# Output projection of a hybrid decoder layer: w_out held in SBUF, x of two quarters kept for the norm, additions on GpSimd, transposes laid between the products

## The chip, the cores and the metric

One core of a Trainium2 chip runs the whole layer. The metric is the device time of one execution in microseconds; the median over the runs of a kernel is given, with the lowest and the highest. A profile is one further execution that the hardware profiler took; its span and its own time stand beside the median below.

## The reference

One decoder layer on x of 2048 rows (tokens) by 1024 columns, all in float32. What matters here are its last steps:

```python
mixed = jnp.concatenate([attn, conv], axis=-1)
x = x + g1 * (mixed @ w_out)

h2 = rmsnorm(x, norm2_g) * (1 + sc2) + sh2
u = causal_dwconv(h2 @ w_up, ffn_conv_w)
u_gate, u_val = jnp.split(u, 2, axis=-1)
y = (jax.nn.silu(u_gate) * u_val) @ w_down
return x + g2 * y
```

`mixed` is 2048 x 1024 (512 columns of attention, 512 of a short convolution), `w_out` 1024 x 1024, `w_up` 1024 x 5632, `w_down` 2816 x 1024. The vectors g1, sc2, sh2, g2 come from the conditioning input and are the same for all rows.

## The kernel before, in words

**Products.** Every float32 product is made of three TensorE matmuls: an operand is split into a high part `hi` (ScalarE, "ACT", L845) and the rest `lo = raw - hi` (VectorE, "DVE", L846), and `mm3` (L139) adds hi·hi, lo·hi and hi·lo into one PSUM accumulator. A matmul here is 128 x 128 by 128 x 512.

**Stages.** The profiled execution runs the projections and the convolution first, then attention (until about 979 us), then the stage of this change, the output projection, until 1208 us, and then the feed-forward part: `up(0)` (1208 to 1634 us), `down` for two quarters, `up(1)`, `down` for the other two.

**The output projection** is `mixed(Q)`, L858, called for four quarters Q of 512 rows. Each has two halves `hf` of 512 output columns. A half goes through eight slices k of 128 rows of w_out, in the order 4, 5, 6, 7, 0, 1, 2, 3; for each k it loads a slice of w_out (L868, 256 KB) into a raw tile (4 buffers), and the matching piece of `mixed`: for k of 4 and over, high and low parts that an earlier stage wrote to DRAM (`m_hi`, `m_lo`, L873 and L874), straight into a pair tile (4 buffers of hi, 4 of lo, taken in turn, so a load waits until TensorE has used the k four places earlier); for k under 4 the attention's output (`m_at`, L870), unsplit. Then come twelve products, three for each of four row tiles t. k = 2 and k = 3 are taken together, t by t. So a half is 96 products in four accumulators, which have four buffers: the next half's accumulator t is the same bank as this one's.

**What follows a half** is `add_gated` (L849) for each t: a load of x (L852), accumulator times gate on DVE (L854), the addition on DVE (L855), the store of the result to x1 in DRAM (L856). Its tiles x and g come from `temp()`, six buffers of 128 x 512 in turn, which all the small steps of this part of the kernel share.

**The norm** `norm2(Q)` (L893) reads x1 of a quarter back (L899), squares it on ACT (L901), scales it on DVE (L906), and for each of eight column blocks makes four transposes on TensorE (L911) and one ACT operation (`columns`, L913). From these come the operands of the up projection: for an even quarter b11 and b21, for an odd one, joined with the even one's by sums and differences on DVE, b22, t1, t2, t3 and t4 (seven products instead of eight). The order is mixed(0), mixed(1), norm2(0), mixed(2), norm2(1), mixed(3), up(0); norm2(2) and norm2(3) lie in `down`.

**The up projection** `up(hv)` (L977) has 22 pairs of column blocks; each pair is seven calls of `product` (L988), twelve matmuls each, in the order b11, t2, b21, t1, t3, b22, t4, into three accumulators X, Y, Z. Between them an accumulator is copied out before the next product is added to it.

**What orders the work.** The program is written in one order, and a scheduler lays the instructions out on each engine by their priority and by when it expects them to be ready; what is wrapped in `K(...)`, like the products of up, keeps its place in the program. In `mixed` the last argument of `mm3`, False, leaves the products free. All loads and stores are issued by SP, one queue.

## Time and profile before

| | |
|---|---|
| median of 3 runs (lowest to highest) | 2562.1 us (2558.01 to 2565.7) |
| profiled execution: its own time, its span | 2563.71 us, 2562.0 us |
| mean granted TensorE clock | 0.988 |
| TensorE busy (matmuls) | 2461.8 us, 96% of the span |
| DVE, ACT, GpSimd busy | 71%, 45%, 12% |
| output projection, 979.65 to 1208.2 us | 228.55 us, TensorE busy 197.21 of it, granted clock 0.93, DMA engines busy 0.83 |
| up(0), 1208.2 to 1634.5 us | 426.3 us, TensorE busy 421.88 of it |

A window's row gives its length, then for each engine the busy time and the number of instructions, then the granted clock as a share of full speed (PEclk), the mean busy share of the sixteen DMA engines, and GB/s. A busy time counts matmuls at whatever clock was granted, so a slow clock does not show as idle time. A row of the waits says which engine and line waited, for which engine (or DMA) and line, how long in total, how often, and the longest. In a timeline a row is a start, a duration, the engine, the line, the instruction and, in brackets, the idle time before it with what ended it; "SPq" rows are issues of DMAs. PE is TensorE, POOL is GpSimd.

### The profile page before, as it was taken

Reading aid. Unit: us, or ns where it says so; the run is one execution under the profiler, and the core shown is the slowest. Engines: PE = TensorE matmul, PEld = TensorE weight load, DVE = VectorE, ACT = ScalarE, POOL = GpSimd, SP = SyncE. Lnnn points to the kernel's source line nnn. Section 1 sums busy time; section 2 is a strip of 40 time slices with the busy share of each in tenths; the row PEclk is TensorE's granted clock in tenths of the full one; section 3 lists DMA queues with packets and bytes.
Section 4 is the critical chain, followed back from the end, with each engine's and each line's share of the span. In section 5 each row is a group of like instructions: output and inputs, shape, how many; then the busy total and the mean of one; then the engine's idle time right before and its main releaser. Section 6 shows DMA issues by size and latency. Waiting matters only on the chain.

```text
span 2562.0 us, 38669 instructions
## 1 busy us (share of the span) xinstructions
PE 2461.8 (96%) x14474; PEld 2030.1 (79%) x14474; DVE 1819.8 (71%) x3266; ACT 1154.9 (45%) x1880; POOL 309.6 (12%) x266
## 2 busy tenths in 40 slices
PE   4999999999999998897999999999999999999999
PEld 4988888887888887675888888877778888888887
DVE  7567874443888884568788888766758888885554
ACT  3532231112888883244444444455434444444333
POOL 4211010112656650000000000000000000000000
PEclk9999999999999999998999999999999999999999
DMA  8433674316799958886222222676642222226776
GB/s 233 144 116 101 194 217 119 118 64 172 141 207 183 178 116 262 298 297 193 83 83 83 83 82 83 201 221 213 215 144 83 83 87 86 75 90 193 224 235 186
DMA packets 423203, 395.97 MB, mean 155 GB/s; under 512 B 136208, under 2 KB 312680, under 8 KB 419944
## 3 DMA queue, kind: packets, MB, share of 16 engines
q1 hardware_dynamic: 415960, 380.86, 51.8%
q10 hardware_dynamic: 7056, 12.65, 1.4%
q8 instruction: 113, 1.85, 0.3%
q14 instruction: 74, 0.61, 0.1%
HBM read 286.41 MB, written 77.66 MB: 142 GB/s over the span
## 4 chain that ended last, share of the span: by engine, by line
PE 51%; DVE 3%; DMA 1%; ACT 1%; issue 1%; SPq 0%; ACTq 0%; DVEq 0%
PE acc L988 33%; PE acc L139 17%; DVE lo L846 1%; DMA raw<-m_at 0%; PE pt L911 0%; DMA t<-x_sc 0%; DVE t L854 0%; DVE t L855 0%; ACT hi L845 0%; DMA t<-in_x_dram 0%; DMA hi<-m_hi 0%; ACT junk L901 0%; ACT t L913 0%; DVE t4l L846 0%; DVE b22l L846 0%
## 5 line engine op out<-in xcount | busy, mean ns | idle before, releaser
L846 DVE TENSOR_TENSOR lo<-raw,hi 128x1024 fp32r<-128x1024 f32 (+1 forms) x240 | 275.4, 1153 | 252.5 <-ACT hi L845 250.3
L845 ACT ACTIVATE hi<-raw 128x1024 fp32r<-128x1024 f32 (+1 forms) x240 | 239.4, 1002 | 375.7 <-PE acc L139 240.6
L139 PE MATMUL acc<-hi 128*128 128x512 f32 x960 | 377.6, 397 | 27.0 <-DVE t L854 11.6
L139 PE MATMUL acc<-lo,hi 128*128 128x512 f32 x960 | 381.0, 397 | 7.6 <-DVE lo L846 7.4
L139 PE MATMUL acc<-hi,lo 128*128 128x512 f32 x960 | 379.7, 396 | 1.5 <-DMA lo<-m_lo 1.5
L1001 DVE SCALAR_TENSOR_TENSOR w<-w,fcw,w 128x1024 f32<-128x1024 f32 x176 | 225.9, 1283 | 35.4 <-ACT w L996 32.1
L139 PEld LDWEIGHTS acc<-hi 128*128 128x128 f32 x960 | 182.3, 190 | 70.5 <-DVE t L854 14.9
L940 ACT ACTIVATE hi<-raw 128x1024 fp32r<-128x1024 f32 x132 | 139.7, 1060 | 211.2 <-PE acc L988 203.0
L139 PEld LDWEIGHTS acc<-lo,hi 128*128 128x128 f32 x960 | 182.6, 190 | 48.1 <-DVE lo L846 11.2
L139 PEld LDWEIGHTS acc<-hi,lo 128*128 128x128 f32 x960 | 183.0, 191 | 40.8 <-DMA lo<-m_lo 3.5
L943 DVE TENSOR_TENSOR lo<-raw,hi 128x1024 fp32r<-128x1024 f32 x132 | 161.0, 1221 | 13.2 <-ACT hi L940 13.2
L704 ACT ACTIVATE s_t<-s_t,nb 128x2048 f32<-128x2048 f32 (+15 forms) x128 | 152.9, 1196 | 5.7
L139 PE MATMUL pr<-hh,wh 128*128 128x512 f32 x384 | 153.3, 399 | 0.0
L139 PE MATMUL pr<-hl,wh 128*128 128x512 f32 x384 | 151.0, 393 | 0.0
L139 PE MATMUL pr<-hh,wl 128*128 128x512 f32 x384 | 150.7, 392 | 0.0
L731 DVE TENSOR_TENSOR near<-pt,near 128x512 f16<-128x512 f32 (+1 forms) x192 | 115.0, 600 | 43.7 <-ACT near L726 42.8
L663 PE MATMUL ps<-kh,qs 128*128 128x512 f32 (+1 forms) x320 | 133.8, 419 | 1.9 <-DVE mx L687 1.1
L687 DVE CUSTOM_DVE_ANT_0 s_t<-ps,nf,mx 128x512 f32<-128x512 f32 (+1 forms) x192 | 123.2, 642 | 2.6
L716 POOL TENSOR_TENSOR wide<-s_t,wide 128x896 f16<-128x896 f32 x64 | 121.5, 1899 | 5.4
L664 PE MATMUL ps<-kl,qs 128*128 128x512 f32 (+1 forms) x320 | 115.5, 365 | 0.0
L724 PE MATMUL pt<-ident,s_t 128*128 128x128 f32 x640 | 101.2, 283 | 6.8 <-DVE near L731 4.4
L139 PE MATMUL acc<-wh,hh 128*128 128x512 f32 x256 | 103.3, 404 | 0.0
(272 smaller groups left out, 6109.0 us busy)
## 6 DMA issues: line engine op xcount, KB each, us to landing
raw<-in_w_up_dram SPq DMA_DIRECT2D x88, 512.0 KB, 3.6
raw<-y_sc SPq DMA_DIRECT2D x176, 256.0 KB, 3.9
raw<-in_w_down_dram SPq DMA_DIRECT2D x176, 256.0 KB, 4.3
y_sc<-w SPq DMA_DIRECT2D x44, 512.0 KB, 2.6
wm<-in_w_ada_dram SPq DMA_DIRECT2D x128, 128.0 KB, 2.7
raw<-in_w_out_dram SPq DMA_DIRECT2D x64, 256.0 KB, 5.7
wr<-in_w_in_dram SPq DMA_DIRECT2D x40, 256.0 KB, 4.2
x_t<-in_x_dram SPq DMA_DIRECT2D x16, 512.0 KB, 5.2
```

What stands on the lines that cost most here:

```text
L139: ins = T.matmul(acc, lhsT=a, rhs=b, start=st, stop=sp)
L663: K(T.matmul(ps[:, 0:cw], lhsT=qt, rhs=kh[:, c0 : c0 + cw], start=True, stop=False))
L664: K(T.matmul(ps[:, 0:cw], lhsT=qt, rhs=kl[:, c0 : c0 + cw], start=False, stop=not last))
L687: K(V.tensor_tensor_reduce(out=s_t[:, o0 + c0 : o0 + c0 + cw], in0=ps[:, 0:cw], in1=nf[:, c0 : c0 + cw], scale=1.0, scalar=-3.0e38 if g == ...
L704: K(A.activation(cols, cols, AF.Exp, bias=nb[:, p : p + 1], accum_out=un["l"][:, p : p + 1]))
L716: K(G.tensor_tensor(wide[:, 1, :], s_t[:, WB * P : WU], wide[:, 0, :], op=ALU.subtract))
L845: A.activation(hi, raw, AF.Copy, scale=HS)
L846: V.tensor_tensor(lo, raw, hi.bitcast(F32), op=ALU.subtract)
L940: K(A.activation(hi, raw, AF.Copy, scale=HS))
L943: K(V.tensor_tensor(lo, raw, hi.bitcast(F32), op=ALU.subtract))
L988: K(T.matmul(acc, lhsT=a, rhs=b, start=st, stop=sp, skip_group_check=True))
L1001: K(V.scalar_tensor_tensor(y, u[:, m : m + 1024], fcw[:, m * 44 + ct : m * 44 + ct + 1], y, op0=ALU.mult, op1=ALU.add))
```

## The change

- **w_out is loaded once.** In mixed(0) the sixteen slices of 128 x 512 (4 MB) go into tiles of a new pool `fb`, which have the names and the buffers that the operands b22 and t4 take later; the other quarters split from there (L847, L848). k under 4 now has two splits of 512 columns, one for w_out and one for m_at, instead of one of 1024, and m_at (L882) is loaded into a tile of `temp()`.
- **x is kept.** The x of quarters 0 and 1 is loaded into four raw tiles and four wide tiles, and the addition is made there in place, so that norm2(0) and norm2(1) read no x1 back. The store to x1 stays.
- **GpSimd** makes the additions of mixed (L858) and the scaling of the norms of quarters 0 and 1 (L943). `temp()` has seven buffers.
- **The products of mixed and the transposes keep their place in the program.** norm2 is a generator now; mixed(1) takes a step of norm2(0) after its first k and then after each k from the sixth on, counted over both halves, and mixed(2) does so with norm2(1).
- **b22 and t4 of quarter 1** need the buffers that hold w_out, so they come after mixed(3): `norm2_rest(1)` makes four steps in the first pair of up(0), after the products b11, t2, b21 and t1, each with four transposes (of columns that mixed(2) has already used for t2 and t3, made a second time), one column on ACT, a split, three operations on DVE for t4 (two before), and a split. norm2(3) makes t4 with the same three operations.

The scheduler then lays out the queues anew from the start of mixed on; before it they are the same. On SP, in the first half of Q1, there stood before (m_at_73 and m_at_74 are k = 2 and 3 of this half, m_hi_75 is the first k of the next; in brackets stands whom an entry waits for, DMAHW being the queues' own counters):

```order
L870 DMA raw<-m_at_73 128x512 [waits DMAHW4_49]
L868 DMA raw<-in_w_out_dram 128x512 [waits DMAHW5_49,Activation_49]
L870 DMA raw<-m_at_74 128x512 [waits DMAHW6_49]
L852 DMA t_13892<-in_x_dram 128x512 [waits DMAHW7_49]
L868 DMA raw<-in_w_out_dram 128x512 [waits DMAHW0_49,DVE_49]
L868 DMA raw<-in_w_out_dram 128x512 [waits DMAHW2_49,DMAHW1_49,DVE_49]
L873 DMA hi<-m_hi_75 128x512 [waits PE_49]
```

All m_at of the half stand ahead of the next half's m_hi. In the same half of the change, on SP (m_hi_76 is the second k of the next half):

```order
L885 DMA hi<-m_hi_75 128x512 [waits DMAHW5_49,DVE_49,PE_49]
L886 DMA lo<-m_lo_79 128x512 [waits DMAHW6_49]
L885 DMA hi<-m_hi_76 128x512 [waits DMAHW7_49,DVE_49,PE_49]
L882 DMA t_13919<-m_at_73 128x512 [waits DMAHW0_49]
L886 DMA lo<-m_lo_80 128x512 [waits DMAHW1_49]
L882 DMA t_13938<-m_at_74 128x512 [waits DMAHW2_49]
```

The m_at of k = 2 and k = 3 have moved behind two m_hi that wait for TensorE. At the end of the first half of Q2 there stands now on SP (m_hi_78 is the fourth k of the next half; the t tiles take x):

```order
L885 DMA hi<-m_hi_78 128x512 [waits DMAHW1_49,DVE_49,PE_49]
L855 DMA t_14462<-in_x_dram 128x512 [waits DMAHW2_49]
L855 DMA t_14468<-in_x_dram 128x512 [waits DMAHW3_49]
L855 DMA t_14474<-in_x_dram 128x512 [waits DMAHW6_49,DMAHW4_49]
L886 DMA lo<-m_lo_82 128x512 [waits DMAHW5_49]
L859 DMA x_sc_91<-t_14462 128x512 [waits Pool_49]
L859 DMA x_sc_92<-t_14468 128x512 [waits DMAHW7_49,Pool_49]
L859 DMA x_sc_93<-t_14474 128x512 [waits DMAHW0_49,Pool_49]
L855 DMA t_14480<-in_x_dram 128x512 [waits DMAHW1_49,DVE_49]
```

The x of the half that ends have moved behind the last m_hi of the next one, where before the first of them stood ahead of the next half's first m_hi. And on ACT, in the first pair of up(0) (t_15154 is the first deferred column, L1073 the copy of the accumulator X):

```order
L918 ACTIVATE t_15154<-pt,sh_141,a_140 128x512 [waits DMAHW1_49,PE_49,Pool_49]
L847 ACTIVATE b22h<-t_15154 128x512 [waits Activation_49]
L847 ACTIVATE t4h<-t_15160 128x512 [waits DVE_49]
L1073 ACTIVATE t_15169<-acc 128x512 [waits DMAHW7_49,DMAHW4_49,Pool_49]
L1078 ACTIVATE w_15171<-halo 128x2
L918 ACTIVATE t_15192<-pt,sh_141,a_140 128x512 [waits DMAHW5_49,PE_49,Pool_49]
```

The copy of X, which before had none of these in front of it, now stands behind the column and two splits.

The diff, cut to its core:

```diff
+NTEMP = 7
...
+        fb = ph.enter_context(tc.tile_pool(name="fb", bufs=1))
...
-        def add_gated(acc, gate, src, dst):
-
-            xp = temp()
+        def add_gated(acc, gate, src, dst, xp=None, eng=V):
+
+            if xp is None:
+                xp = temp()
             nc.sync.dma_start(xp, src)
             g = temp()
             V.tensor_tensor(g, acc, gate, op=ALU.mult)
-            V.tensor_tensor(xp, xp, g, op=ALU.add)
+            eng.tensor_tensor(xp, xp, g, op=ALU.add)
             nc.sync.dma_start(dst, xp)
 
-        def mixed(Q):
+        wo, kept = {}, {}
+
+        def mixed(Q, side=iter(()), wait=0):
 
             cols = slice(Q * 512, (Q + 1) * 512)
+            n = 0
+            if Q == 0:
+                kept[0] = [raw_tile() for _ in range(4)]
+                kept[1] = [wide_temp()[:, 0:D] for _ in range(4)]
             for hf in range(2):
                 n0 = hf * 512
                 acc = [ps_d.tile([P, 512], F32, tag="d", name="acc") for _ in range(4)]
                 ops = []
                 for k in (4, 5, 6, 7, 0, 1, 2, 3):
-                    raw, tiles = raw_tile(), pair_tiles()
-                    (mh, ml), (wh, wl) = halves(tiles)
-                    nc.sync.dma_start(raw[:, 512:1024], w_out[k * P : (k + 1) * P, n0 : n0 + 512])
+                    if Q == 0:
+                        wo[k, hf] = fb.tile([P, 512], F32, tag=f"{('b22', 't4')[k // 4]}{k % 4}{'hl'[hf]}", name="wo")
+                        nc.sync.dma_start(wo[k, hf], w_out[k * P : (k + 1) * P, n0 : n0 + 512])
+                    (mh, ml), (wh, wl) = halves(pair_tiles())
+                    split(wo[k, hf], wh, wl)
                     if k < 4:
-                        nc.sync.dma_start(raw[:, 0:512], m_at[k][:, cols])
-                        split(raw, *tiles)
+                        raw = temp()
+                        nc.sync.dma_start(raw, m_at[k][:, cols])
+                        split(raw, mh, ml)
                     else:
                         nc.sync.dma_start(mh.bitcast(F32), m_hi[k - 4][:, cols])
                         nc.sync.dma_start(ml.bitcast(F32), m_lo[k - 4][:, cols])
-                        split(raw[:, 512:1024], wh, wl)
                     ops.append((mh, ml, wh, wl))
                     for t in () if k == 2 else range(4):
                         for o in ops:
                             a, b = [m[:, t * P : (t + 1) * P] for m in o[:2]]
-                            mm3(acc[t], a, b, *o[2:], k == 4, o is ops[-1] and k == 3, False)
+                            mm3(acc[t], a, b, *o[2:], k == 4, o is ops[-1] and k == 3)
                     if k != 2:
                         ops = []
+                    n += 1
+                    if n == 1 or n > wait:
+                        next(side, None)
                 for t in range(4):
                     r = Q * 4 + t
-                    add_gated(acc[t], gates[:, n0 : n0 + 512], x[r * P : (r + 1) * P, n0 : n0 + 512], x1_sc[r][:, n0 : n0 + 512])
+                    xp = kept[Q][t][:, n0 : n0 + 512] if Q < 2 else None
+                    add_gated(
+                        acc[t], gates[:, n0 : n0 + 512], x[r * P : (r + 1) * P, n0 : n0 + 512], x1_sc[r][:, n0 : n0 + 512], xp, G
+                    )
 
         bt = {}
 
         def operand(name, k, raw):
-            bt[name, k] = [fp.tile([P, 512], F32R, tag=f"{name}{k}{e}", name=f"{name}{e}") for e in "hl"]
+            pool = fb if name in ("b22", "t4", "t3") else fp
+            bt[name, k] = [pool.tile([P, 512], F32R, tag=f"{name}{k}{e}", name=f"{name}{e}") for e in "hl"]
             split(raw, *bt[name, k])
...
+        xn = {}
+
+        def columns(Q, k):
+            pt = ps_n.tile([P, 512], F32, tag="n", name="pt")
+            for t in range(4):
+                K(T.transpose(pt[:, t * P : (t + 1) * P], xn[Q][t][:, k * P : (k + 1) * P], ident))
+            h = temp()
+            A.activation(h, pt, AF.Identity, bias=sh2[:, k : k + 1], scale=a2[:, k : k + 1])
+            return h
+
+        def last_operands(Q, k, b2):
+            b21, t2 = bt["b21", k], bt["t2", k]
+            operand("b22", k, b2)
+            t4, t5 = temp(), temp()
+            V.tensor_tensor(t4, b21[0].bitcast(F32), t2[0].bitcast(F32), op=ALU.subtract)
+            V.tensor_tensor(t5, b21[1].bitcast(F32), t2[1].bitcast(F32), op=ALU.subtract)
+            V.tensor_tensor(t4, t4, t5, op=ALU.add)
+            operand("t4", k, t4)
+
         def norm2(Q):
 
             ss = fp.tile([P, 16], F32, tag="ss", name="ss", bufs=2)[:, 0:4]
-            xn = []
+            xn[Q] = kept.get(Q) or [wide_temp()[:, 0:D] for _ in range(4)]
             for t in range(4):
-                xt = wide_temp()[:, 0:D]
-                nc.sync.dma_start(xt, x1_sc[Q * 4 + t])
-                junk = fp.tile([P, D], BF16, tag="t2", name="junk", bufs=6)
-                A.activation(junk, xt, AF.Square, accum_out=ss[:, t : t + 1])
-                xn.append(xt)
+                if Q >= 2:
+                    nc.sync.dma_start(xn[Q][t], x1_sc[Q * 4 + t])
+                junk = fp.tile([P, D], BF16, tag="t2", name="junk", bufs=NTEMP)
+                A.activation(junk, xn[Q][t], AF.Square, accum_out=ss[:, t : t + 1])
             V.tensor_scalar(ss, ss, 1.0 / D, EPS, op0=ALU.mult, op1=ALU.add)
             rsqrt(fp, ss, 4, "r")
             for t in range(4):
-                V.tensor_scalar(xn[t], xn[t], ss[:, t : t + 1], None, op0=ALU.mult)
-
-            def columns(k):
-                pt = ps_n.tile([P, 512], F32, tag="n", name="pt")
-                for t in range(4):
-                    T.transpose(pt[:, t * P : (t + 1) * P], xn[t][:, k * P : (k + 1) * P], ident)
-                h = temp()
-                A.activation(h, pt, AF.Identity, bias=sh2[:, k : k + 1], scale=a2[:, k : k + 1])
-                return h
-
+                if Q < 2:
+                    G.tensor_scalar(xn[Q][t], xn[Q][t], ss[:, t : t + 1], 0.0, op0=ALU.mult, op1=ALU.add)
+                else:
+                    V.tensor_scalar(xn[Q][t], xn[Q][t], ss[:, t : t + 1], None, op0=ALU.mult)
+            yield
             for k in range(4):
-                b1, b2 = columns(k), columns(4 + k)
                 if Q % 2 == 0:
-                    operand("b11", k, b1)
-                    operand("b21", k, b2)
+                    for n, name in enumerate(("b11", "b21")):
+                        operand(name, k, columns(Q, 4 * n + k))
+                        yield
                     continue
-                operand("b22", k, b2)
-                b11, b21 = [[e.bitcast(F32) for e in bt[n, k]] for n in ("b11", "b21")]
-                t1, t2, t3, t4 = [temp() for _ in range(4)]
+                b1 = columns(Q, k)
+                b11 = [e.bitcast(F32) for e in bt["b11", k]]
+                t1, t2, t3 = [temp() for _ in range(3)]
                 V.tensor_tensor(t1, b1, b11[0], op=ALU.subtract)
                 V.tensor_tensor(t1, t1, b11[1], op=ALU.subtract)
                 operand("t1", k, t1)
+                yield
+                b2 = columns(Q, 4 + k)
                 V.tensor_tensor(t2, b2, t1, op=ALU.subtract)
                 operand("t2", k, t2)
                 V.tensor_tensor(t3, b2, b1, op=ALU.subtract)
                 operand("t3", k, t3)
-                V.tensor_tensor(t4, b21[0], t2, op=ALU.subtract)
-                V.tensor_tensor(t4, t4, b21[1], op=ALU.add)
-                operand("t4", k, t4)
+                if Q == 3:
+                    last_operands(Q, k, b2)
+                yield
+
+        def norm2_rest(Q):
+            for k in range(4):
+                last_operands(Q, k, columns(Q, 4 + k))
+                yield
...
-        def up(hv):
+        def up(hv, side):
...
                 product(X, o11, "b11", True)
+                next(side, None)
...
                 product(Y, os2, "t2", True)
+                next(side, None)
...
                 product(X, o12, "b21", False)
+                next(side, None)
...
                 product(Z, os1, "t1", True)
+                next(side, None)
...
         mixed(0)
-        mixed(1)
-        norm2(0)
-        mixed(2)
-        norm2(1)
+        mixed(1, norm2(0), 5)
+        mixed(2, norm2(1), 5)
         mixed(3)
         for hv in range(2):
-            up(hv)
+            up(hv, iter(()) if hv else norm2_rest(1))
             for n in range(4):
                 down(2 * hv + n // 2, n % 2)
                 if hv == 0 and n < 2:
-                    norm2(2 + n)
+                    for _ in norm2(2 + n):
+                        pass
```

More of the change, by code (lines that the diff above doesn't have):

```diff
@@ L838, in temp @@
         def temp():
-            return fp.tile([P, 512], F32, tag="t2", name="t2", bufs=6)
+            return fp.tile([P, 512], F32, tag="t2", name="t2", bufs=NTEMP)
         def wide_temp():
```

## The prediction

> **What bounds the kernel now.** I read the page first, then windows cut at the ends of the halves of the output projection, then the waits of TensorE in that stage, then single timelines. The windows are the eight halves (Q0 first half, Q0 second half, and so on), and the whole stage last.
>
> ```profile
> core 0: us, PE busy (x) PEld busy (x) DVE busy (x) ACT busy (x) POOL busy (x), PEclk, DMA share, GB/s
> 979.65:1001.40 21.75, 21.75 (x92) 17.84 (x91) 9.51 (x11) 7.27 (x9) 0.00 (x0) 0.92 0.86 288
> 1001.40:1025.90 24.50, 22.66 (x97) 17.63 (x96) 12.64 (x17) 6.78 (x8) 0.00 (x0) 1.00 0.86 278
> 1025.90:1051.40 25.50, 22.94 (x97) 17.59 (x96) 12.24 (x16) 6.77 (x8) 0.00 (x0) 1.00 0.90 296
> 1051.40:1075.30 23.90, 22.68 (x97) 17.62 (x97) 11.55 (x15) 5.40 (x6) 0.00 (x0) 1.00 0.88 307
> 1075.30:1112.20 36.90, 28.88 (x129) 21.91 (x129) 23.97 (x44) 21.60 (x34) 0.00 (x0) 0.86 0.86 280
> 1112.20:1138.20 26.00, 23.27 (x98) 17.59 (x97) 12.03 (x17) 6.78 (x8) 0.00 (x0) 1.00 0.89 300
> 1138.20:1186.40 48.20, 33.23 (x138) 25.30 (x137) 43.88 (x79) 28.80 (x46) 0.00 (x0) 0.84 0.64 207
> 1186.40:1208.20 21.80, 21.80 (x94) 17.89 (x92) 12.22 (x16) 5.31 (x5) 0.00 (x0) 0.96 0.92 289
> ...
> 979.65:1208.20 228.55, 197.21 (x832) 153.37 (x830) 138.04 (x208) 88.70 (x124) 0.00 (x0) 0.93 0.83 273
> ```
>
> A half without gaps takes 21.8 us. Two halves, those with the norm between them, take 36.9 and 48.2. In 228.55 us TensorE is busy 197.2 and idle 31.3; the granted clock of 0.93 costs another 228.55 × 0.07 = 16. So 181 us is work at full clock, and 47 us could be won at most. Who makes TensorE wait (total, times, longest):
>
> ```profile
> PE acc L139 <- DVE t L854: 11.0, 3, 8.7
> PE acc L139 <- ACT hi L845: 7.9, 1, 7.9
> PE acc L139 <- DMA hi<-m_hi: 5.1, 5, 1.9
> PE acc L139 <- DVE lo L846: 4.4, 5, 2.9
> PE acc L988 <- DVE lo L943: 4.4, 1, 4.4
> ```
>
> The 8.7 and the 7.9 belong to the norms (DVE's chain, and Squares that wait for the reloaded x1). The last row is the first pair of the up projection. What a wait costs beside itself shows behind that one. The first two rows below are TensorE's timeline, the others windows of 3.4 us from there:
>
> ```profile
> 1208.10 0.39 PE L988 MATMUL acc<-b11l,hi 128*128 128x512 f32 x1
> 1212.91 0.79 PE L988 MATMUL acc<-b11h,lo 128*128 128x512 f32 x1 [4.42 <-DVE lo L943]
> ```
> ```profile
> 1211.60:1215.00 3.40, 2.09 (x5) 1.71 (x6) 3.24 (x5) 0.72 (x2) 0.00 (x0) 0.58 0.10 36
> 1215.00:1218.40 3.40, 3.40 (x9) 2.63 (x9) 2.36 (x2) 2.20 (x5) 0.00 (x0) 0.50 0.09 25
> 1218.40:1221.80 3.40, 3.40 (x15) 2.75 (x15) 0.68 (x2) 0.00 (x0) 0.00 (x0) 0.92 0.92 271
> ```
>
> After 4.42 us idle the clock is 0.58, 0.50 and 0.92 in three windows: (0.42 + 0.50 + 0.08) × 3.4 = 3.4 us lost again. I take 3.4 for waits of 4 to 6 us, and half, 1.7, for waits of 2 to 3 (an estimate).
>
> One more view decides the forecast: the timeline of SP, which issues all the loads, around 1138.2, where a half ends.
>
> ```profile
> 1130.88 0.32 SPq L873 DMA_DIRECT2D hi<-m_hi  x1
> 1131.25 0.42 SPq L874 DMA_DIRECT2D lo<-m_lo  x1
> 1131.73 1.25 SPq L852 DMA_DIRECT2D t<-in_x_dram  x1
> ...
> 1138.25 0.33 SPq L856 DMA_DIRECT2D x_sc<-t  x1
> 1138.67 0.38 SPq L873 DMA_DIRECT2D hi<-m_hi  x1
> ...
> 1140.84 1.03 SPq L856 DMA_DIRECT2D x_sc<-t  x2
> ...
> 1142.48 0.43 SPq L873 DMA_DIRECT2D hi<-m_hi  x1
> ```
>
> The m_hi load at 1130.88 goes into a pair tile (4 buffers, 8 k per half) and so waits until TensorE is through with the k four places earlier, 7.3 us before the half's end; the x load behind it goes out right after, never before. The m_hi of 1142.48 stands behind the stores of 1140.84. SP's queue is taken in order, and a load waits for the entries ahead of it.
>
> **The change part by part.** Prices:
>
> ```profile
> raw<-m_at SPq DMA_DIRECT2D x32, 256.0 KB, 5.0
> t<-in_x_dram SPq DMA_DIRECT2D x32, 256.0 KB, 3.7
> ...
> hi<-m_hi SPq DMA_DIRECT2D x28, 256.0 KB, 4.5
> ```
> ```profile
> L846 DVE TENSOR_TENSOR lo<-raw,hi 128x1024 fp32r<-128x1024 f32 x32 | 39.0, 1224 | 48.3 <-ACT hi L845 46.2 <-DMA raw<-in_w_out_dram 1.6
> ...
> L854 DVE TENSOR_TENSOR t<-acc,gates 128x512 f32<-128x512 f32 x32 | 21.9, 688 | 11.6 <-PE acc L139 11.5
> ...
> L845 ACT ACTIVATE hi<-raw 128x512 fp32r<-128x512 f32 x29 | 18.3, 630 | 44.3 <-PE acc L139 25.0 <-DMA raw<-in_w_out_dram 15.0 <-DMA t<-in_x_dram 4.1
> L913 ACT ACTIVATE t<-pt,sh,a 128x512 f32<-128x512 f32 x16 | 12.3, 768 | 3.3 <-PE pt L911 3.0 <-DMA raw<-m_at 0.3
> ```
> ```profile
> L274 POOL TENSOR_TENSOR hl<-hf,hh 128x512 fp32r<-128x512 f32 x8 | 10.4, 1297 | 0.7
> ...
> L263 POOL TENSOR_SCALAR x_t<-x_t,ss 128x1024 f32<-128x1024 f32 x2 | 3.2, 1604 | 2.6 <-DVE ss L126 2.6
> ```
>
> *What goes.* The w_out loads of Q1 to Q3 and the x1 reloads of two norms; the bulk of the norms' work is laid between products. The 7.9 and the 8.7, and the clock behind them, end. Work stays 181; the first half's clock (0.92 of 21.75 = 1.7) stays, and I leave 3 us for small waits at the ends of halves. Stage without new waits: 186. Splitting k < 4 in two pieces adds instructions on DVE and ACT, which are busy half of a half; the scalings (4 × 1.6 us, twice) lie on GpSimd, beside products. Both I cost at nothing; were the scalings late, transposes would wait about 1 us, in places where TensorE waits anyway.
>
> *What comes: m_at behind m_hi.* The first two groups of rows of SP's queue that stand with the change show Q1's first half. Before, all m_at of the half stood ahead of the next half's m_hi. Now m_hi_76 waits until TensorE has done k = 1, and m_at_73, which TensorE needs next, goes out only then. TensorE waits about 0.4 (issue) + 3.7 (landing, the x row; 5.0 is m_at's own at a DMA share near 0.9, and traffic falls) + 0.63 (hi on ACT) less transposes in between: 4.5 us, with bounds 3 and 6. The same stands in Q1's second half, and in both of Q2. Four times 4.5 + 3.4 = 32 us.
>
> *x loads behind the half's end.* The third group shows SP at the end of Q2's first half. The first three x go out only when TensorE has finished the half (T); before, the first x stood ahead of m_hi_75. x lands at T + 4.2, GpSimd adds until T + 5.5 (1.30), which frees a temp for the third gate product on DVE, done at T + 6.2: only then is the third accumulator free, which TensorE wants at T + 1.4 (six of 96 products of a 21.8 us half). The fourth comes one add and one product later, 1.3 us more than TensorE's 0.7. Together 6 us, and 3.4 of clock: 9.4. At both ends of Q3's first half an m_lo load stands behind two stores that wait for GpSimd: 2.5 + 1.7 each, 8.4 in all (bounds 0 and 6 each).
>
> Stage: 186 + 32 + 9.4 + 8.4 = 236, against 228.5: **+7**.
>
> *First pair of the up projection.* Here stand the sixteen deferred transposes with four columns; the fourth group of rows shows ACT. The copy of the first accumulator (L1073), for which TensorE's third product waits, stands behind t4h, and so behind four operations of DVE. Twelve products take an eighth of 21.8, 2.7 us; 64 transposes take 181 − 8 × 21.8 = 7 us in the stage, four of them 0.45. From the end of the first four transposes to that of the copy (taken like a column, 0.77): 0.77 + 0.63 + 4 × 0.69 + 0.63 + 0.77 = 5.6, against 2.7 + 0.45 of other work: 2.4 us idle. At the fourth group the copy of the third accumulator stands so too: 5.6 against 2.7, 2.9 idle. Transposes 1.8 us; the first wait is 3.3 (four gate products done 0.7 after the end, two sums and one split of 1.22) instead of 4.4 and a few tenths; clock 3 × 1.7. Sum 15.5 (3.3 + 1.8 + 2.4 + 2.9 + 5.1), against 4.4 + 3.4 + 0.5 (from 1208.1 to the second row of the pair shown above is 4.8): **+7**.
>
> *norm2(3).* One operation more for each t4, 4 × 0.69 = 2.8 us, where DVE is full:
>
> ```profile
> 1790.00:1815.00 25.00, 22.03 (x101) 17.13 (x100) 24.39 (x36) 18.39 (x26) 0.00 (x0) 1.00 0.47 136
> ```
>
> TensorE waits 3 us there already; I take **+2** (0 to 4).
>
> Sum: 7 + 7 + 2 = +16 on the profiled execution's 2563.7 (span 2562.0), 2580; it lay 1.6 above the median of the runs, so **2578**.
>
> *GpSimd against DVE.* An add of 1.30 us replaces one of 0.69, and runs while DVE subtracts. The L274 row has 1297 ns, while DVE's operations on 512 columns stay at 688; nothing in these rows shows a lock. The Trainium skill ("SBUF — State Buffer", section "Who interferes with whom") says that a DVE instruction with two inputs in SBUF and a GpSimd instruction that reads SBUF share a port pair, and one blocks the other; by that rule the sum would be the third rival's, 2602.
>
> **The rivals.** *Short landing, no change* (chance 0.2): loads land in 2 to 3 us now that w_out is gone; each m_at wait is 3 + 1.7, the x chain 4 + 1.7, Q3's waits vanish. Stage 186 + 19 + 6 = 211; −17.5, and +9 behind it: 2554, the edge of no change; with half of that shortening 2566. For: DMA share falls. Against: x landed in 3.7 at shares near 0.9 already. It decides at a landing under 3 us.
>
> *The loads aren't late, faster* (0.2): TensorE runs late enough elsewhere, or temps come free so, that m_at lands before it is wanted; then the stage is 186 to 195 and the total 2528 to 2538. For: 47 us lie there. Against: the wait is on the very k before. It decides if no m_at wait is over 1 us.
>
> *GpSimd blocks DVE, slower still* (0.15): 32 adds of 1.30 and 8 scalings of 1.6 hold DVE's splits at each of the half ends; at 3 us on the path in each of eight halves, 24 more: 2602.
>
> **How the numbers follow.** My forecast has 0.45. No change is ±0.3%, 7.7 us, about what can be measured here: 2554 to 2570. Slower 0.45 + 0.15 = 0.6, same 0.2, faster 0.2. The bounds of the terms (four waits ±1.5 each, Q3, up, norm) give 2562 to 2596 for the likeliest; with half of the fast rival and most of the slow one the range is 2540 to 2602.
>
> **What would show it.** Right: in the waits of the changed kernel, TensorE waits for ACT's hi or DVE's lo from an m_at temp, 3 to 6 us, four times, in Q1 and Q2, and 5 us on L857 early in Q2's second half; granted clock near 0.85 in these halves; the first pair near 31 us instead of 24.3. Wrong: halves of Q1 and Q2 at 22 to 24 us, a stage under 200, or waits of that size for another engine.

## The result, and the profile after

The changed kernel takes 2590.87 us (median of 4 runs, 2587.15 to 2591.12) against 2562.71 us of the kernel before in the same comparison (2558.01 to 2565.7): a ratio of 1.0108, 95% interval 1.009 to 1.0126. It is slower by 28 us, where the forecast was 16 (2578), and inside the forecast's range of 2540 to 2602. The profiled spans are 2589.4 and 2562.0 us, 27.4 apart, and that is divided as follows.

| stretch | before, us | after, us | difference | forecast |
|---|---|---|---|---|
| up to the output projection | 979.65 | 979.60 | 0 | 0 |
| output projection | 228.2 | 246.2 | +18.0 | +7 |
| up(0) | 426.4 | 433.7 | +7.3 | +7 |
| all that follows | 927.7 | 929.9 | +2.2 | +2 |

The rows are read from the timelines of TensorE by the first product of each stage; in the kernel before, that of up(0) is at 1207.87, and five products of the output projection had run before 979.65, in gaps of attention. The windows of the changed kernel, with the output projection and then the first pair of up(0):

```profile
979.60:1225.78 246.18, 205.42 (x836) 160.26 (x834) 118.39 (x186) 90.79 (x148) 53.44 (x38) 0.91 0.57 184
1225.78:1259.63 33.85, 25.35 (x101) 19.30 (x100) 30.09 (x41) 15.98 (x26) 3.81 (x2) 0.90 0.22 69
```

and the first pair of the kernel before, cut in the same way (from the first product of one pair to that of the next):

```profile
1207.87:1234.45 26.58, 22.16 (x85) 17.74 (x84) 18.09 (x24) 8.31 (x14) 0.00 (x0) 0.87 0.22 70
```

The DMA engines' share in the output projection fell from 0.83 to 0.57 and DVE's busy time from 138 to 118 us, as the change is made to do. TensorE is idle 246.18 − 205.42 = 40.8 us there, where it was 31.3, and the granted clock of 0.91 costs 22 us, where it was 16. Less traffic and less work on DVE, and more waiting. Who it waits for (total, times, longest; L1026 is the up projection):

```profile
PE acc L140 <- ACT hi L847: 22.5, 6, 6.1
PE acc L140 <- DMA lo<-m_lo: 8.5, 3, 4.5
PE acc L140 <- DVE t L857: 7.4, 7, 2.4
...
PE acc L1026 <- DVE lo L981: 3.4, 2, 2.9
PE acc L1026 <- ACT t L1073: 1.8, 1, 1.8
```

The 8.7 on DVE's norm and the 7.9 on ACT behind the reload of x1 are gone. In their place stands the high part of an m_at tile, six times. On TensorE's timeline the stage's waits of over 2 us are these (start, duration, instruction, and in brackets the idle time before it):

```profile
1047.50 0.50 PE L140 MATMUL acc<-hi 128*128 128x512 f32 x1 [2.54 <-ACT hi L847]
...
1072.09 0.50 PE L140 MATMUL acc<-hi 128*128 128x512 f32 x1 [2.13 <-ACT hi L847]
1080.38 0.79 PE L140 MATMUL acc<-hi 128*128 128x512 f32 x1 [4.48 <-ACT hi L847]
...
1113.36 0.79 PE L140 MATMUL acc<-hi 128*128 128x512 f32 x1 [3.44 <-ACT hi L847]
1124.90 0.50 PE L140 MATMUL acc<-hi 128*128 128x512 f32 x1 [2.28 <-DVE t L857]
1129.98 0.79 PE L140 MATMUL acc<-hi 128*128 128x512 f32 x1 [2.45 <-DVE t L857]
...
1149.24 0.50 PE L140 MATMUL acc<-hi 128*128 128x512 f32 x1 [3.86 <-ACT hi L847]
1160.70 0.79 PE L140 MATMUL acc<-hi 128*128 128x512 f32 x1 [6.07 <-ACT hi L847]
1181.16 0.79 PE L140 MATMUL acc<-hi,lo 128*128 128x512 f32 x1 [4.46 <-DMA lo<-m_lo]
1208.16 0.68 PE L140 MATMUL acc<-hi,lo 128*128 128x512 f32 x1 [3.33 <-DMA lo<-m_lo]
```

The first, third, fourth and sixth wait for ACT are the four forecast places. In the second halves (the third and the sixth) the late tile is k = 1, behind the next half's first m_hi, and not k = 2 behind its second. The first of the four on SP's timeline:

```profile
1040.02 0.43 SPq L886 DMA_DIRECT2D lo<-m_lo  x1
1042.37 0.32 SPq L885 DMA_DIRECT2D hi<-m_hi  x1
1042.73 0.43 SPq L882 DMA_DIRECT2D t<-m_at  x1
```

TensorE issues the last product of k = 1 at 1041.95; the m_hi that waits for it goes out at 1042.37, and the m_at behind it at 1042.73. Was the m_at held by its buffer? Its temp had been read last by GpSimd's fourth addition of the half before:

```profile
1026.76 1.67 POOL L858 TENSOR_TENSOR raw<-raw,t 128x512 f32<-128x512 f32 x1 [1.23 <-DVE t L857]
```

It was free at 1028.4, 14 us before the load went out. Only the place in the queue kept it. At the other three places the temps had been free for 13, 15 and 9 us when the loads went out (last use until 1062.8, 1093.8 and 1146.0, loads at 1075.9, 1108.7 and 1155.1).

The second and the fifth wait, 2.13 and 3.86 us, have another cause. They are for m_at of k = 0 in the second halves of Q1 and Q2. The load for the second went out at 1063.24 and had landed by 1067.3, but its split on ACT began only at 1071.42, behind a column and a split (b11h) of the norm, which wait for the four transposes just ahead of these products:

```profile
1070.88 0.63 ACT L847 ACTIVATE b11h<-t 128x512 fp32r<-128x512 f32 x1
1071.42 0.61 ACT L847 ACTIVATE hi<-t 128x512 fp32r<-128x512 f32 x1
```

The load for the fifth did wait for its temp. It went out as soon as DVE had read that temp for the last time, in a subtraction of the norm (L961, until 1144.06); it had landed by 1147.1, and its split stood behind one of the norm's:

```profile
1143.37 0.69 DVE L961 TENSOR_TENSOR t<-t,t 128x512 f32<-128x512 f32 x1
```
```profile
1144.08 0.32 SPq L882 DMA_DIRECT2D t<-m_at  x1
```
```profile
1148.04 0.63 ACT L847 ACTIVATE t1h<-t 128x512 fp32r<-128x512 f32 x1 [1.54 <-DVE t L957]
1148.58 0.61 ACT L847 ACTIVATE hi<-t 128x512 fp32r<-128x512 f32 x1
```

### The profile page after: what moved, and what is told of

Its sections match the earlier page's. It is cut to its first block, busy times and chain, and to the rows that moved or that the text cites. A ratio compares the mean times of both kernels' runs of the same rounds, so it can differ in the third digit from the quotient of the medians.

```text
span 2589.4 us, 38682 instructions
## 1 busy us (share of the span) xinstructions
PE 2473.2 (96%) x14490; PEld 2039.3 (79%) x14490; DVE 1813.5 (70%) x3266; ACT 1166.2 (45%) x1916; POOL 367.1 (14%) x306
## 4 chain that ended last, share of the span: by engine, by line
PE 51%; DVE 2%; DMA 2%; ACT 1%; issue 0%; SPq 0%; POOL 0%; ACTq 0%; DVEq 0%
PE acc L1026 32%; PE acc L140 18%; DMA t<-x_sc 1%; DVE lo L848 1%; PE pt L916 0%; ACT hi L847 0%; DMA lo<-m_lo 0%; DMA out_dram<-t 0%; DMA raw<-in_w_down_dram 0%; DVE t L857 0%; DVE t L858 0%; DVE raw L975 0%; DMA t<-m_at 0%; DVE lo L981 0%; DVE t L925 0%
## 5 line engine op out<-in xcount | busy, mean ns | idle before, releaser
L140 PE MATMUL acc<-hi 128*128 128x512 f32 x960 | 383.9, 401 | 30.1 <-ACT hi L847 22.5
L848 DVE TENSOR_TENSOR lo<-raw,hi 128x1024 fp32r<-128x1024 f32 x176 | 214.7, 1224 | 186.0 <-ACT hi L847 185.5
L847 ACT ACTIVATE hi<-raw 128x1024 fp32r<-128x1024 f32 x176 | 186.0, 1061 | 261.5 <-PE acc L140 209.4
L978 ACT ACTIVATE hi<-raw 128x1024 fp32r<-128x1024 f32 x132 | 139.7, 1060 | 213.4 <-PE acc L1026 202.9
L981 DVE TENSOR_TENSOR lo<-raw,hi 128x1024 fp32r<-128x1024 f32 x132 | 161.0, 1221 | 10.7 <-ACT hi L978 10.7
L848 DVE TENSOR_TENSOR lo<-wo,hi 128x512 fp32r<-128x512 f32 x64 | 51.8, 812 | 78.8 <-ACT hi L847 78.4
```

Source lines behind the costliest of these rows:

```text
L140: ins = T.matmul(acc, lhsT=a, rhs=b, start=st, stop=sp)
L847: A.activation(hi, raw, AF.Copy, scale=HS)
L848: V.tensor_tensor(lo, raw, hi.bitcast(F32), op=ALU.subtract)
L978: K(A.activation(hi, raw, AF.Copy, scale=HS))
L981: K(V.tensor_tensor(lo, raw, hi.bitcast(F32), op=ALU.subtract))
```

## The experiments

Two theories stood at the start. Theory 1: loads and stores stand in SP's queue behind entries that wait for TensorE or GpSimd. Theory 2: GpSimd's additions block DVE, so that its splits come late. Each run was timed against the kernel before on its own chip (medians 2561.4 to 2562.3 us). A difference between two changed kernels is the difference of their medians, also where they ran on different chips. Lengths of the output projection and of the first pair of up(0) are from the profiled executions, by first products.

**Own buffers for m_at.**

```diff
-                        raw = temp()
+                        raw = raw_tile()[:, 0:512] if Q > 1 else fb.tile([P, 512], F32, tag=f"t3{k}{'hl'[hf]}", name="ma")
```

> Only the tiles that m_at is loaded into are changed (buffers of t3 in Q0 and Q1, raw tiles in Q2 and Q3, instead of the shared temps), and with that every m_at load stands ahead of the next half's m_hi loads in SP's queue. Theory 1 (loads queued behind entries that wait for TensorE): the six waits of TensorE for ACT's hi on L847, 22.5 us in the changed kernel, fall under 4 us, and most of the slow clock behind them goes (about 3 us for each of five places): 30 to 38 us faster than the changed kernel, 2553 to 2561. The waits for L857 at the start of Q2's second half (5.5 us) stay. Theory 2 (GpSimd's additions block DVE, whose splits come late): nothing moves, 2588 to 2594.

2556.45 us, ratio 0.9974 (0.9964 to 0.9983): 34 us faster than the changed kernel. The waits of TensorE:

```profile
PE acc L140 <- DMA lo<-m_lo: 7.7, 5, 3.2
PE acc L140 <- DVE t L857: 7.1, 7, 2.3
```

No wait for L847 is left of 22.5 us, and the waits for L857 stay. The other 12 us are clock: the output projection takes 212.2 us at 0.95, where it was 246.2 at 0.91. Theory 1 holds with its number. The scheduler lays out all the engines' queues anew with the edit, so the two waits with another cause go as well: on ACT the split of m_at now stands ahead of the norm's.

**Additions on DVE.**

```diff
-                        acc[t], gates[...], x[...], x1_sc[...], xp, G
+                        acc[t], gates[...], x[...], x1_sc[...], xp, V
```

> The additions of the output projection go back to DVE, all else as in the changed kernel. Theory 1 (the queue): the chain of x, addition and gate product at the start of Q2's second half is 0.6 us shorter for each addition, the rest stays, since m_at stands where it stood: 0 to 6 us faster than the changed kernel, 2585 to 2591. Theory 2 (GpSimd blocks DVE, or its additions are what TensorE waits for): 15 to 25 us faster, 2566 to 2576.

2577.28 us, ratio 1.0059 (1.0047 to 1.0072): 13.6 us faster than the changed kernel, between the two theories. Of the waits the six for L847 stay; those for m_lo go:

```profile
PE acc L140 <- ACT hi L847: 22.4, 6, 5.3
...
PE acc L140 <- DMA lo<-m_lo: 2.1, 4, 1.0
...
PE acc L1026 <- ACT t L1073: 0.3, 1, 0.3
```

I had counted only the shorter addition. The stores that wait for it stand in front of m_lo loads in the queue, so 6.4 us of those waits go too, with their clock: the output projection takes 236.3 us instead of 246.2. That the stores do it was a guess until the tenth run. The other 4 us lie in the first pair of up(0), 29.9 us instead of 33.9. There the changed kernel has, on GpSimd and on DVE:

```profile
1228.20 3.81 POOL L858 TENSOR_TENSOR t<-t,t 128x512 f32<-128x512 f32 x2 [2.82 <-DMA x_sc<-t]
```
```profile
1229.23 1.65 DVE L975 TENSOR_TENSOR raw<-t,raw 128x512 f32<-128x512 f32 x1
1230.91 1.65 DVE L975 TENSOR_TENSOR raw<-raw 128x512 f32<-128x512 f32 x1
```

With the additions on DVE each of these two sums takes 0.69 us, 1.9 us less for both. TensorE's waits in the pair fall by 2.1 us, from 8.5 to 6.4, and the rest is clock. So theory 2 is right in part: in that pair GpSimd's additions hold up DVE. What else the move changes there no run separates.

**The copies first.** p1 and p5 are written ahead of the deferred step:

```diff
-                next(side, None)
                 p1 = temp()
                 K(A.activation(p1, X, AF.Copy))
+                next(side, None)
...
```

> In the first pair of the up projection the copies of the accumulators X and Z (p1 and p5) are written ahead of the deferred step, not behind it. Theory 1 (the copies stand behind the deferred splits in ACT's queue): the waits of 1.8 us for L1073 and 3.1 us for L1096 go, with 2 to 3 us of clock: 4 to 8 us faster than the changed kernel, 2583 to 2587. Rival (the deferred work fills ACT and DVE in the pair, whatever its order): the waits turn up at a later product of the pair, under 2 us are won.

2589.15 us, 1.7 us less than the changed kernel, which this many runs cannot tell from none. The rival holds: the wait for the copy of X is gone, that for the copy of Z stays at 3.2 us, and a new one of 1.1 us for DVE's sum (L974) stands behind it.

**x early in Q2 and Q3 too.** With own buffers for m_at, the raw tile's other half takes x:

```diff
+                        if Q > 1:
+                            both = raw_tile()
+                            raw, xs[k] = both[:, 0:512], both[:, 512:1024]
+                            nc.sync.dma_start(xs[k], x[(Q * 4 + k) * P : (Q * 4 + k + 1) * P, n0 : n0 + 512])
```

> As the kernel with own buffers for m_at, and in Q2 and Q3 x too is loaded into the second half of those raw tiles, ahead of the products of its half, not behind them. Theory 1: the waits for L857 at the start of Q2's second half (5.5 us) and most of the waits for m_lo in Q3 (7.8 us) go as well, with the clock behind them: 10 to 20 us faster than the kernel with own buffers for m_at alone, 2538 to 2550. Rival (the accumulators are freed late because DVE or GpSimd are late, not x): under 3 us faster than that kernel.

2555.27 us, ratio 0.9976 (0.9966 to 0.9987), 1.2 us faster than with own buffers alone. This is the rival's number, but not its cause: the waits for the gate product fell from 7.1 to 3.5 us, and a new one took the gain. The raw tiles are held by x until the stores of Q3, and the first weights of up(0) come late:

```profile
PE acc L1032 <- ACT hi L984: 6.3, 1, 6.3
PE acc L140 <- DVE t L858: 3.5, 3, 2.3
```

**Own buffers and additions on DVE.** The first two edits together.

> Own buffers for m_at and the additions on DVE, both edits at once. Theory 1, with what the single edits showed (34 and 14 us): the stores of a half no longer wait for GpSimd's additions in front of the m_lo loads, so the two waits for m_lo in Q3 (3.0 and 3.25 us with own buffers) fall under 1 us and the clock behind them comes back; the gains add, 2540 to 2547. Rival (the gain of the additions on DVE came from other places of m_at in the queue, which own buffers have mended already): 2552 to 2557.

2547.05 us, ratio 0.994 (0.9928 to 0.9953). The gain is 9.4 us on top of own buffers, at the edge of the range; the waits for m_lo fell from 7.7 to 2.9 us, one of 2.6 remains in Q3.

**The same, and x of Q2 early.** As in the fourth run, for Q2 alone.

> As the kernel with both edits, and x of Q2 is loaded early into the second half of the raw tiles of m_at; in Q3 x stays in temps, so that the raw tiles come free for the up projection's weights. Theory 1 (x is late at the start of Q2's second half): the waits for the gate product there, 5.3 us with own buffers, fall under 2.5, with 2 to 3 us of clock: 4 to 8 us faster than the kernel with both edits, 2533 to 2541. Rival (raw tiles are freed late by the stores, so m_at of Q2's second half is late instead): no faster than the kernel with both edits.

2541.32 us (2537.52 to 2542.34), ratio 0.992 (0.9907 to 0.9934): 5.7 us faster than with the two edits, faster than both kernels. The window of the output projection, which begins at 978.10 in this execution:

```profile
978.10:1176.43 198.33, 187.36 (x835) 150.36 (x834) 128.13 (x217) 88.05 (x148) 12.71 (x8) 0.99 0.70 229
```

The stage takes 198 us instead of 228 and 246; the clock is 0.99 in it. But the gain came from another place than theory 1 gave. At the start of Q2's second half the waits for the gate product went from 2.34 and 1.59 us with the two edits to 2.34, 0.84 and 0.35, hardly less; the m_lo wait of 2.6 us in Q3 is what went (0.8 us for m_lo in all). Why the first wait does not move shows DVE's timeline in the changed kernel:

```profile
1122.20 1.38 DVE L848 TENSOR_TENSOR lo<-wo,hi 128x512 fp32r<-128x512 f32 x2 [7.07 <-ACT hi L847]
1123.56 0.69 DVE L956 TENSOR_TENSOR t<-t,b11h 128x512 f32<-128x512 f32 x1
1124.16 0.68 DVE L857 TENSOR_TENSOR t<-acc,gates 128x512 f32<-128x512 f32 x1
...
1129.23 0.69 DVE L857 TENSOR_TENSOR t<-acc,gates 128x512 f32<-128x512 f32 x1 [2.39 <-POOL t L858]
1131.68 0.69 DVE L857 TENSOR_TENSOR t<-acc,gates 128x512 f32<-128x512 f32 x1 [1.76 <-POOL t L858]
```

The first gate product stands behind two splits for the next half and a step of the norm, and these wait for ACT, which waits for a tile that TensorE frees at the half's end. Only the third and the fourth wait for GpSimd, and so for x.

**The norms between the quarters.** norm2(0) runs through after mixed(1), norm2(1) after mixed(2); no step lies in a half:

```diff
-        mixed(1, norm2(0), 5)
-        mixed(2, norm2(1), 5)
+        mixed(1)
+        for _ in norm2(0):
+            pass
+        mixed(2)
+        for _ in norm2(1):
+            pass
```

> The norms of the first two quarters stand between the quarters, as before the change, not between the products; all else as in the changed kernel. Theory 1a (m_at comes late in the queue because the columns and sums of the norm take the shared temps): with no norm steps in a half, the m_at loads stand ahead of the m_hi loads, the waits for L847 fall under 4 us, and in their place come two norms by themselves, 8 to 12 us each with their clock: 2568 to 2582. Theory 1b (m_at comes late because the products keep the program's order): the waits stay and the norms come on top, 2605 to 2620.

2591.03 us, ratio 1.0111 (1.0097 to 1.0125), the time of the changed kernel and neither theory's number. The waits tell them apart all the same:

```profile
PE pt L916 <- ACT t L918: 12.7, 14, 1.1
PE pt L916 <- POOL w L943: 11.1, 4, 9.2
PE pt L916 <- POOL raw L943: 10.4, 4, 8.5
```

No wait for L847 is left, with m_at in the same seven temps and the products pinned as before: it is the norm's steps that put the m_at loads late. The two norms cost 34 us of waits, not the 16 to 24 that I gave them. GpSimd scales four tiles one after the other, and each group of transposes waits for one ACT operation. So against this arrangement the transposes between products save some 34 us and their clock, and the order that comes with them spends it again. In the kernel before, whose norms scale on DVE, the norm's waits were 16.6 us (8.7 and 7.9).

**Without b22 and t4.** The deferred steps are left out; the products use t3's tiles.

> The four deferred steps in the first pair of the up projection are left out: for the first two quarters the products with b22 and t4 use t3's tiles in their place, so the output differs and only the time is read. Theory 1 (the deferred steps cost the first pair 7 us): 6 to 10 us faster than the changed kernel, 2581 to 2585. Rival (the pair waits for its weights' splits all the same): under 3 us faster.

2579.7 us, ratio 1.0073 (1.0058 to 1.0087): 11 us faster than the changed kernel, a little over the range. Without them the pair waits only for its weights (L981, 3.4 us), as it did before the change for 4.4. The pair takes 25.3 us instead of 33.9, so the steps cost 8.6 us in it, a little more than the 7.3 by which it became longer.

**m_at on ACT's queue.**

```diff
-                        nc.sync.dma_start(raw, m_at[k][:, cols])
+                        nc.scalar.dma_start(raw, m_at[k][:, cols])
```

> The m_at loads of the changed kernel are issued by ACT instead of SP; buffers, additions and products are as in the changed kernel. Theory 1 (what costs is that m_at stands behind other entries of SP's queue, not that its temp is late): the waits for L847, 22.5 us, fall under 8, and the kernel is 15 to 35 us faster than the changed one, 2556 to 2576. Rival (the temps come free too late, and own buffers cured that): the waits stay above 15 us, 2582 to 2595.

2606.81 us, ratio 1.0179 (1.0165 to 1.0192): neither number. The waits for L847 rose:

```profile
PE acc L140 <- ACT hi L847: 29.5, 8, 5.8
```

The load of k = 2 in Q1's first half now stands on ACT behind the column whose transposes follow k = 1 on TensorE:

```
L918 ACTIVATE t_13909<-pt,sh_141,a_140 128x512 [waits PE_49]
L882 DMA t_13919<-m_at_73 128x512 [waits DMAHW1_49]
```

The edit moved the loads from behind one entry that waits for TensorE to behind another. So it does not separate the queue from the temps. What separates them is when the temps came free in the changed kernel: 9 to 15 us early at the four forecast places, where the queue alone kept the loads, and just then at the fifth wait.

**Stores on GpSimd's queue.** With own buffers for m_at and the additions on GpSimd:

```diff
-            nc.sync.dma_start(dst, xp)
+            (nc.sync if eng is V else nc.gpsimd).dma_start(dst, xp)
```

> Own buffers for m_at; the additions stay on GpSimd, and the stores behind them are issued by GpSimd instead of SP. Theory 1 (the additions on GpSimd cost because the stores wait for them in SP's queue, ahead of m_lo): the waits for m_lo in Q3 (6.2 us) fall under 2.5, and the time comes near that of the additions on DVE: 2544 to 2551. Theory 2 (they cost because GpSimd and DVE block one another: splits of up to 1.86 us instead of 0.69): no gain, 2552 to 2560.

2547.74 us, ratio 0.9944 (0.9932 to 0.9957): the time of the additions on DVE (2547.05), with the additions still on GpSimd. No wait for m_lo is left among TensorE's seven largest. But the equal times hide two differences. The output projection takes 197.7 us, where it takes 204.8 with the additions on DVE (fifth run) and 212.2 with the additions on GpSimd and the stores on SP (first run); the first pair of up(0) takes 37.4, where it takes 31.6 and 33.9. In that pair DVE's first two sums run beside additions on GpSimd (1179.57 and 1181.72, 1.27 us each), and TensorE waits for the split behind them, 5.79 us instead of 2.86 in the first run:

```profile
1179.21 2.19 DVE L974 TENSOR_TENSOR t<-raw 128x512 f32<-128x512 f32 x1
1181.44 2.11 DVE L975 TENSOR_TENSOR raw<-raw 128x512 f32<-128x512 f32 x1
```
```profile
1184.74 0.80 PE L1026 MATMUL acc<-b11h,lo 128*128 128x512 f32 x1 [5.79 <-DVE lo L981]
```

The two sums take 2.9 us more than at 0.69 each, and that is what the wait is longer by. So in the output projection the additions on GpSimd cost through the stores that wait for them in SP's queue, and theory 1 holds there; in the first pair they cost by holding up DVE, as theory 2 has it. No run has the additions on DVE with the stores off SP's queue.

**x early, additions on GpSimd.** The sixth kernel with that one edit undone.

> The fastest kernel so far (own buffers, x of Q2 early, additions on DVE), with the additions back on GpSimd. Theory 1: the stores that wait for GpSimd in SP's queue and the longer chain to the gate products cost as they did with own buffers alone: 6 to 11 us slower than the fastest, 2547 to 2552. Theory 2 (blocking alone costs, and it hits splits that TensorE does not wait for): under 3 us slower, 2540 to 2544.

2551.35 us, ratio 0.9963 (0.9951 to 0.9975), 10 us slower than the sixth; the waits for m_lo are 7.3 us instead of 0.8. This is theory 1's number.

**The fastest, copies first.**

> The fastest kernel so far, with the copies p1 and p5 ahead of the deferred steps. In it the wait for p5 (2.4 us) is the longest of the first pair but one. Theory 1: that wait goes with 1 to 2 us of clock, 2 to 4 us faster, 2537 to 2540. Rival (as in the changed kernel: the wait turns up at the next product): within 2 us of the fastest, 2539 to 2543.

2544.53 us, ratio 0.9931 (0.9916 to 0.9945), 3 us slower than the sixth if anything; the intervals overlap. The wait for the copy of Z is 3.0 us, and one of 2.1 for DVE's sum has come; the first pair takes 34.3 us instead of 30.2. It is the rival in kind: the wait turns up elsewhere.

## Why the prediction was right, point by point

- **Work at full clock, 181 us.** Now 205.42 − 22 = 183. Held.
- **m_at behind m_hi, four waits of 4.5 us.** They are 2.5, 4.5, 3.4 and 6.1: 16.5 us against 18, with temps that had long been free. Held, and the first run, which puts m_at ahead, takes all of it away.
- **The term that was put at nothing.** Two further waits for ACT's hi, 2.1 at 1072.09 and 3.9 at 1149.24, are the m_at of k = 0 in the second halves of Q1 and Q2. The prediction let the norm's work between products cost nothing. But at the first place the split of m_at stands on ACT behind the norm's column and split, and at the second the norm holds the temp that the load needs, and then ACT: 6 us with no term of their own.
- **x behind the end of Q2's first half, 6 us.** 2.28 + 2.45 and one more of 0.81 = 5.5 us. The size held, the cause for 3.3 of it: the last two are x and GpSimd, as forecast. The 2.28 is DVE's order: the gate product behind splits and a norm step that wait for the half's end themselves, which the prediction had not seen, and it stays when x is early (2.34 in the sixth run).
- **m_lo behind stores in Q3, 2.5 each.** 4.5 and 3.3: 2.8 us more. The tenth run, which takes the stores out of SP's queue, shows the mechanism by itself.
- **Clock, 13.6 + 3.4 + 3.4 + 1.7 = 22 us.** 22 measured, but in part by luck: the waits were longer in sum (40.8 us of idle time against 32 in the prediction), so each cost less than its price, and the 1.7 for the first half did not come at all (1.00 in both halves of Q0). In the four halves of Q1 and Q2, where 0.85 was forecast, the clock was 0.95, 0.90, 0.89 and 0.79. The stage came out 246 instead of 236 by the 6 us without a term, 3 on m_lo, 2 of work and 2 of small waits, less 2 on the forecast waits for m_at and x.
- **First pair of up(0), +7.** 33.85 against 26.58: +7.3, and as much over the whole of up(0). (The 24.3 and 31 of the prediction are of a window that ends 2 us before the next pair.) The waits in it are 2.9, 0.5, 1.8 and 3.1 where 3.3, 2.4 and 2.9 were forecast. But the 2.4 was reckoned with DVE's operations at 0.69 us. With the additions on DVE, where they do take that, the wait for the copy of X is 0.3 us and the pair takes 29.9 (second run): 4 of the 7.3 us go with GpSimd's additions beside DVE, which the prediction put at nothing. That the sum agrees so well is in part luck. Writing the copies first wins next to nothing (third and twelfth run): DVE and ACT have the work to do in that pair, and the next product waits.
- **norm2(3), +2.** All that follows up(0) is 2.2 us longer. No run took it alone.
- **GpSimd blocks DVE.** As a price of 24 us at the ends of halves the rival fell, as a mechanism it stood. The splits of w_out on DVE in the output projection, first with additions on GpSimd (the changed kernel), then on DVE (second run); count, shortest, median and longest in ns:

```profile
L848 DVE TENSOR_TENSOR lo<-wo,hi x62: 675/693/1864, 978.8 to 1215.8; 128x512 fp32r<-128x512 f32 x62
```
```profile
L848 DVE TENSOR_TENSOR lo<-wo,hi x61: 678/691/894, 982.1 to 1206.2; 128x512 fp32r<-128x512 f32 x61
```

The gate product in the changed kernel, whose one input is in PSUM:

```profile
L857 DVE TENSOR_TENSOR t<-acc,gates x31: 677/691/693, 998.3 to 1224.6; 128x512 f32<-128x512 f32 x31
```

Some splits take 1.2 us longer beside an addition on GpSimd; the product never does. The Trainium skill, "SBUF — State Buffer", section "Who interferes with whom", says that a DVE instruction with two inputs in SBUF and a GpSimd instruction that reads SBUF exclude one another, and that one with at most one input in SBUF, outside the modes in which DVE takes both ports, does not meet GpSimd; this trace agrees with both, 1864 ns and 693 ns. The prediction read no lock in the rows of before. The trace of before has one, beside the very L274 that the prediction took its price from. L232 adds to an accumulator in SBUF; its shortest, median and longest in ns, then six of them in a row and GpSimd beside them:

```profile
L232 DVE SCALAR_TENSOR_TENSOR acc<-wa,cact,acc x48: 471/476/1580, 14.0 to 57.5; 128x256 f32<-128x256 f32 x48
```
```profile
27.41 5.17 DVE L232 SCALAR_TENSOR_TENSOR acc<-wa,cact,acc 128x256 f32<-128x256 f32 x6
```
```profile
28.05 1.31 POOL L274 TENSOR_TENSOR hl<-hf,hh 128x512 fp32r<-128x512 f32 x1
30.20 1.31 POOL L274 TENSOR_TENSOR hl<-hf,hh 128x512 fp32r<-128x512 f32 x1
```

Six at the median would take 2.9 us. In the output projection the lock cost nothing that can be seen: with the stores on GpSimd's own queue it takes 197.7 us, with the additions on DVE and x early 198.3. In the first pair of up(0), with the clock behind it, it cost up to 4 us (second run).

The gain that the change is made for is there: the 16.6 us of norm waits of before, and the clock behind them, are covered, and with the queue mended the stage is 198 us. In the changed kernel it was lost to loads that the queue held behind entries that wait, to the norm's work on ACT and in the shared temps, and to the clock behind each of these waits.

## What to carry to other kernels

Before work is laid between products, look at the queue that issues the loads: a load that is ready can stand behind one that waits for the very product ahead of it, and tiles shared with the new work are enough to put it there. Give loads that a stage needs next buffers of their own, and keep stores that wait for a slow engine off the queue that feeds TensorE. When work goes to GpSimd, look at what DVE does beside it. Equal times of two kernels can hide a gain in one stage and a loss in the next, so compare them by stage. In the output projection here 40.8 us of waits came with 22 us lost to the clock, about half as much again.

## What the runs showed of the hardware

DVE operations of 128 x 512 with both inputs in SBUF, 0.69 us alone, took longer beside GpSimd additions: a subtraction (L848) up to 1.86 us and a sum (L975) 1.65 in the changed kernel, a sum (L974) 2.19 in the tenth run. A product with one input in PSUM (L857) stayed at 0.69. GpSimd's additions (L858) took 1.26 to 2.13 us in the changed kernel.

Loads that SP issues went out in the order of its queue: one whose tile had been free for 9 to 15 us still stood behind a load that waited for TensorE.
